# Loading the input transposed, warming TensorE ahead of the first products, and four small edits in a one-core diffusion step

## The chip, the cores and the metric

The kernel runs on one core of a Trainium2 chip. The metric is device time in microseconds (us). The kernel before takes 435.55 us, the median of 3 runs (435.24 to 435.67). The profile shown below is of one further execution that took 436.31 us, of which the profiler's span covers 434.5 us.

## What is computed

One layer of a hybrid mixer works on 640 tokens of 1024 channels: 128 context tokens and 512 latent tokens. Cut to what this change touches, the reference is

```python
mod = silu(c) @ w_ada + b_ada                  # c_ctx for context, c for latent tokens
shift, scale, gate = split(mod, 3)
h = rmsnorm(x, g_pre) * (1 + scale) + shift    # 640 x 1024
proj = h @ w_in                                # 3840 columns: qa ka va ga qr zf zb ir gr uf gf
# neighbourhood attention (8 heads), bidirectional gated recurrence (4 heads), Fourier mixing,
# each times a gate taken from proj, then
y = x + gate * rmsnorm(mixed @ w_out, g_post)
```

The outputs are y, the new keys and values of the context tokens, and the final states of the recurrence. The scale and shift that a channel gets depend only on which of the two groups its token belongs to, so they are two numbers a channel each.

## The kernel before

Everything is float32. A weight or vector that goes into a big product is split into a high part (rounded to the fast float32 format, by ScalarE) and a low part (the rest, by VectorE), and a product is the sum of three fast products: high by high, high by low, low by high (`mm3`, line 210). In the products the channels lie on the partitions, in KT = 8 tiles of 128 channels; `hT[0]` and `hT[1]` (line 203) hold the high and low parts of the modulated input, 128 channels by 640 tokens for each of the 8 tiles.

**The first stage** is `start_stream` (line 244). It loads x as five tiles of 128 tokens, each in a piece of 640 columns (`xa`) and one of 384 (`xb`), on SyncE's queue, and behind them the 16 modulation weights `wss` of 512 KB, with the first two blocks of the input projection (`win`) in between. `scale_x` (line 222) takes the sum of squares of a token from ScalarE (line 225) and VectorE (line 226), its root and reciprocal (lines 164 and 165), and scales the tile (lines 230 and 231). Then, for each channel tile k:

- `mod_cols` (line 195) forms scale and shift of 128 channels from two weight blocks, as 8 narrow products each (128x32 by 128x128, two records of the profile for one product);
- VectorE copies the result out of PSUM into `row` (line 266), TensorE transposes it (line 270), VectorE adds up (line 272) and makes `G` (lines 273 and 274) and `shift` (line 275);
- `modulated` (line 233) transposes five 128x128 pieces of x on TensorE into PSUM, ScalarE applies `G` and `shift` to them (line 237 for the latent tokens, line 239 for the context tokens), and VectorE writes the high part (line 240) and the low part (line 241) of `hT`.

`zf_stream` (line 283) follows tile by tile: 12 products of 320 columns for each k, into four PSUM banks, which `gate` (line 321) empties with two sigmoids each when the eighth k is in. `fill` (line 958) starts after the fifth tile and runs all other blocks of the projection in a list, one block being 48 such products.

**The later stages** overlap: two recurrences (`recurrence`, line 416; VectorE updates over seven levels, then the states, line 525), four attentions, the Fourier part and the output projection. `attention_blocks(p)` (line 574) projects values, transposes the five 128-token tiles of the values with `by_token` (line 343) into two PSUM banks, four tiles in a bank of the kind "b" and the fifth in one of the kind "f" (of which there are three, and in which the blocks accumulate), and splits them into `vs` (line 632). The gate of the output is made in `gate_vectors` (line 846), which uses a small constant `sel`.

**What sets the order.** The functions are generators; a planner (`Order`) with estimated costs interleaves them, and that gives the program order. Within it the framework's scheduler orders each engine's instructions by a simulated timeline. SyncE's loads are chained in the order of `wdma`; each engine's queue runs strictly in its order. SyncE has up to eight loads under way and then waits for an earlier one to land.

Of the kernel before, what the change touches and what calls it, by code (L numbers as in the profile page):

```python
# [9 lines left out]
F32 = mybir.dt.float32  # L10
# [3 lines left out]
ALU = mybir.AluOpType  # L14
# [3 lines left out]
P = 128  # L18
# [53 lines left out]
def mixer_kernel(ctx: ExitStack, tc: tile.TileContext, A, O):  # L72
# [51 lines left out]

    def tr(out, src):
        od.now += 0.107
        last_tr[0] = te.transpose(out, src, ident).ins  # L127

    def split(src, hi, lo, hi_eng=None, lo_eng=None):
        (sc.copy if hi_eng is None else hi_eng.tensor_copy)(hi, src)  # L130
        (ve if lo_eng is None else lo_eng).tensor_sub(lo, src, hi.bitcast(F32))  # L131
# [41 lines left out]
    wdma, nb = [], [1]  # L173
# [7 lines left out]
    def split_w(raw, lo_eng=None, shape=(KT, P), tags=("hi", "lo")):  # L181
        hi, lo = [wp.tile([P, *shape], F32R, tag=t, name=nm(t), bufs=WB[t]) for t in tags]
        split(raw, hi, lo, lo_eng=lo_eng)
        return hi, lo
# [10 lines left out]
    def mod_cols(out, w, chain):  # L195

        t = od.now
        for k in range(KT):
            run_mm(chain, out[32 * (k % 4):32 * (k % 4) + 32, :], csil[:, k, :], w[:, k, :], start=(k < 4), stop=(k >= 4))
        od.now = t + 0.45  # L200
# [3 lines left out]
    xa, xb = [T(tag="xa") for _ in range(5)], [T(384, tag="xb") for _ in range(5)]  # L204

    def xcols(i, k):
        return (xa[i] if k < 5 else xb[i])[:, k % 5 * P:k % 5 * P + P]
# [9 lines left out]
    def load_x():  # L217
# [4 lines left out]
    def scale_x():  # L222
        for i in range(5):
            ss2 = S(2)
            sc.activation(T(), xa[i], ACT.Square, accum_out=ss2[:, 0:1])
            ve.tensor_tensor_reduce(PE_()[:, 0:384], xb[i], xb[i], 1.0, 0.0, op0=ALU.mult, op1=ALU.add,
                                    accum_out=ss2[:, 1:2])
            ve.tensor_add(rstd[:, i:i + 1], ss2[:, 0:1], ss2[:, 1:2])
            rsqrt_mean(rstd[:, i:i + 1], D)
            ve.tensor_scalar(xa[i], xa[i], rstd[:, i:i + 1], 0.0, op0=ALU.mult, op1=ALU.add)  # L230
            ve.tensor_scalar(xb[i], xb[i], rstd[:, i:i + 1], 0.0, op0=ALU.mult, op1=ALU.add)

    def modulated(k, pm):
        h, px = T(), PB()
        for i in range(1, 5):
            tr(px[:, (i - 1) * P:i * P], xcols(i, k))
        sc.activation(h[:, P:NT], px, ACT.Identity, bias=shift[:, k, 1:2], scale=G[:, k, 1:2])
        tr(pm[:, 384:512], xcols(0, k))
        sc.activation(h[:, 0:P], pm[:, 384:512], ACT.Identity, bias=shift[:, k, 0:1], scale=G[:, k, 0:1])
        ve.tensor_copy(hT[0][:, k, :], h)  # L240
        ve.tensor_sub(hT[1][:, k, :], h, hT[0][:, k, :].bitcast(F32))
        od.set(f"h{k}", LAT["h"])

    def start_stream():
        load_x()
# [10 lines left out]
        scale_x()  # L256
        od.now = 11.0
        for k in range(KT):
# [7 lines left out]
            ve.tensor_copy(row, pm[:, 0:256])  # L266
            yield LAT["row"]

            for u in range(2):
                tr(pm[:, u * P:(u + 1) * P], row[:, u * P:(u + 1) * P])  # L270
            pt = S(4)
            ve.reduce_sum(pt, pm[:, 0:256].rearrange("p (u g r) -> p u r g", u=2, r=32)[:, :, 0:2, :], axis=AX.X)
            ve.tensor_scalar(G[:, k, :], pt[:, 0:2], bss[:, k, 0:1], 1.0, op0=ALU.add, op1=ALU.add)
            ve.tensor_scalar_mul(G[:, k, :], G[:, k, :], gpre[:, k:k + 1])  # L274
            ve.tensor_scalar_add(shift[:, k, :], pt[:, 2:4], bss[:, k, 1:2])
            modulated(k, pm)
# [66 lines left out]
    def by_token(src):  # L343
# [4 lines left out]
        return [(slice(4 * j, 4 + j), pt[j][:, 0:(4, 1)[j] * P].rearrange("p (i e) -> p i e", e=P)) for j in range(2)]  # L348
# [225 lines left out]
    def attention_blocks(p):  # L574
# [54 lines left out]
        vp = by_token(vT)  # L629
# [216 lines left out]
    def gate_vectors():  # L846
        selr = cp.tile([P, 2, P], F32R, tag="selr", name="selr")
# [219 lines left out]
def prepare(inp):  # L1067
    inp = {k: np.asarray(v) for k, v in inp.items()}
    r = _consts()
    r["x"] = np.concatenate([inp["x_prompt"][0], inp["x_sample"][0]], 0)  # L1070
    r["cc"] = np.stack([inp["c_ctx"], inp["c"][0]], -1).reshape(KT, P, 2).transpose(1, 0, 2)
# [59 lines left out]
```

## Time and profile before

| | |
|---|---|
| median of 3 runs | 435.55 us |
| profiled execution | 436.31 us, span 434.5 us |
| TensorE busy (modelled) | 410.3 us, 94% |
| VectorE busy | 303.2 us, 70% |
| ScalarE busy | 204.7 us, 47% |
| first product of TensorE | 14.27 us |
| read from memory | 43.80 MB |

PE is TensorE, PEld its weight loads, DVE VectorE, ACT ScalarE, POOL GpSimd, SP SyncE. In the groups of instructions a row reads: line, engine, operation, output<-input, shapes, count | busy time, mean ns of one | idle time of the engine just ahead of it and what ended that. The rows by stretch of time give, for each engine, the busy time and the count of instructions, then the granted clock of TensorE, the busy share of the DMA engines and GB/s. The chain of waits is followed back from the last instruction; a row there is a start, a length and the engine with the tile it writes. In the timeline the first two columns are start and length, and a bracket tells how long the engine had been idle and what released it.

### The profile page before, as it was taken

The numbers are of one execution on the slowest core, as the hardware profiler recorded it, in microseconds if no ns is written. First come the engines' busy times: TensorE is split into PE (matmuls) and PEld (weight loads), VectorE is DVE, ScalarE is ACT, GpSimd is POOL, SyncE is SP. The second block draws the span as 40 slices with busy tenths as digits, with TensorE's granted clock in tenths as the row PEclk, the third lists the DMA queues.
The fourth block names the chain that finished last, engine by engine and source line by source line (L and its number), as shares of the span: only waits on it lengthen the run. The fifth ranks groups of instructions, "written<-read, shape, count | busy, mean of one in ns | idle before, by whom it ended". The sixth has DMA issues, their size and how long they took to land.

```text
span 434.5 us, 8311 instructions
## 1 busy us (share of the span) xinstructions
PE 410.3 (94%) x3176; PEld 373.0 (86%) x3176; DVE 303.2 (70%) x866; ACT 204.7 (47%) x546; POOL 7.4 (2%) x23
## 2 busy tenths in 40 slices
PE   0699999999998999999999999999999999999994
PEld 0388899999988998999899989899898889988884
DVE  2775479999986865885597658786679748471164
ACT  5524467575341525654454534744456553251231
POOL 2000000000020100000000000000000000000000
PEclk9999999999999999999999999999999999999999
DMA  7996143211202011132112423245324203245032
GB/s 241 411 407 228 49 154 116 66 55 50 84 23 74 13 60 50 56 97 66 40 61 67 146 67 92 93 152 181 100 55 141 98 1 105 76 160 205 0 146 98
DMA packets 19528, 47.62 MB, mean 110 GB/s; under 512 B 3184, under 2 KB 6912, under 8 KB 19488
## 3 DMA queue, kind: packets, MB, share of 16 engines
q1 hardware_dynamic: 19376, 46.94, 31.7%
q8 instruction: 25, 0.41, 0.4%
q0 software_dynamic: 112, 0.14, 0.3%
q14 instruction: 15, 0.12, 0.1%
HBM read 43.80 MB, written 3.28 MB: 108 GB/s over the span
## 4 chain that ended last, share of the span: by engine, by line
PE 90%; DVE 4%; DMA 3%; ACT 1%; issue 1%; SPq 0%; DVEq 0%; ACTq 0%
PE pb L113 83%; PE pb L127 6%; DMA vs<-wss 1%; DMA txa<-x 1%; DVE AL L451 1%; DVE t L525 1%; DVE AL L488 0%; ACT L681 0%; DVE lo L131 0%; DVE t L953 0%; ACT hi L130 0%; ACT pe L682 0%; DVE t L468 0%; DVE t L467 0%; DVE AC L451 0%
## 5 line engine op out<-in xcount | busy, mean ns | idle before, releaser
L113 PE MATMUL pb<-hT,hi 128*128 128x320 f32 x896 | 209.5, 317 | 3.0 <-DVE vs L131 1.5
L113 PEld LDWEIGHTS pb<-hT,hi 128*128 128x128 f32 x896 | 149.4, 188 | 9.5 <-issue 2.3
L113 PE MATMUL pb<-hT,lo 128*128 128x320 f32 x448 | 139.0, 312 | 0.0
L113 PEld LDWEIGHTS pb<-hT,lo 128*128 128x128 f32 x448 | 84.1, 188 | 1.0 <-DVE G L274 0.2
L131 DVE TENSOR_TENSOR lo<-raw,hi 128x1024 fp32r<-128x1024 f32 x35 | 42.8, 1223 | 26.9 <-ACT hi L130 26.5
L130 ACT CAST hi<-raw 128x1024 fp32r<-128x1024 f32 x35 | 36.8, 1051 | 41.9 <-PE pb L113 20.9
L113 PE MATMUL pb<-t,t 64*128 64x128 f32 (+2 forms) x414 | 43.1, 291 | 0.4 <-DVE AL L451 0.4
L113 PEld LDWEIGHTS pb<-t,t 64*128 64x128 f32 (+1 forms) x414 | 36.2, 188 | 4.8 <-issue 0.8
L130 ACT CAST pT<-pb 128x256 fp32r<-128x256 f32 x64 | 23.3, 372 | 19.3 <-DVE pT L131 12.3
L113 PE MATMUL pb<-hi,mh 128*128 128x512 f32 (+1 forms) x108 | 32.1, 376 | 0.0
L131 DVE TENSOR_TENSOR pT<-pb,pT 128x256 fp32r<-128x256 f32 x64 | 26.4, 418 | 1.7 <-ACT pT L130 1.5
L113 PEld LDWEIGHTS pb<-hi,mh 128*128 128x128 f32 x108 | 19.4, 189 | 3.2
L113 PE MATMUL pb<-pT,mh 128*128 128x512 f32 (+1 forms) x102 | 22.2, 364 | 0.0
L681 ACT ACTIVATE pe<-pb,s 128x256 f32<-128x256 f32 x32 | 15.3, 477 | 13.8 <-DVE s L680 7.9
L127 PE MATMUL pb<-ident,pe 128*128 128x128 f32 x136 | 20.9, 273 | 0.5 <-ACT pe L682 0.5
L113 PEld LDWEIGHTS pb<-pT,mh 128*128 128x128 f32 x102 | 17.7, 189 | 3.1
L936 ACT ACTIVATE t<-pb 128x512 f32<-128x512 f32 (+1 forms) x11 | 6.0, 551 | 30.1 <-PE pb L113 30.1
L113 PE MATMUL pb<-lo,mh 128*128 128x512 f32 (+1 forms) x54 | 20.2, 373 | 0.0
L127 PEld LDWEIGHTS pb<-ident,pe 128*128 128x128 f32 x136 | 16.6, 140 | 1.4 <-ACT pe L682 0.7
L451 DVE COPY_PREDICATED AL<-masks,pb 128x512 f32<-128x512 uint32 x24 | 16.5, 738 | 1.5 <-PE pb L113 1.5
L113 PE MATMUL pb<-pT,vs 128*128 128x256 f32 (+1 forms) x96 | 16.8, 321 | 0.0
L113 PE MATMUL pb<-vs,csil 128*32 128x128 f32 x64 | 3.3, 335 | 14.3 <-DMA vs<-wss 14.3
(205 smaller groups left out, 636.3 us busy)
## 6 DMA issues: line engine op xcount, KB each, us to landing
raw<-win SPq DMA_DIRECT2D x30, 512.0 KB, 3.5
pT<-wss SPq DMA_DIRECT2D x12, 512.0 KB, 10.2
raw<-wg SPq DMA_DIRECT2D x8, 512.0 KB, 3.5
raw<-wout SPq DMA_DIRECT2D x8, 512.0 KB, 3.5
t<-x SPq DMA_DIRECT2D x10, 256.0 KB, 6.1
o_y<-t SPq DMA_DIRECT2D x9, 256.0 KB, 2.1
vs<-wss SPq DMA_DIRECT2D x4, 512.0 KB, 9.3
tbl<-tbl SPq DMA_DIRECT2D x4, 512.0 KB, 3.5
```

The costliest lines, as they stand in the source:

```text
L113: return te.matmul(out, lhsT, rhs, start=start, stop=stop).ins
L127: last_tr[0] = te.transpose(out, src, ident).ins
L130: (sc.copy if hi_eng is None else hi_eng.tensor_copy)(hi, src)
L131: (ve if lo_eng is None else lo_eng).tensor_sub(lo, src, hi.bitcast(F32))
L451: ve.copy_predicated(out, mk.to_broadcast([P, i1 - i0, P]), src)
L525: ve.scalar_tensor_tensor(sall[r, cdst], sall[r, cs], Td[r, ip:ip + 1], pst[r, cdst], op0=ALU.mult, op1=ALU.add)
L681: sc.activation(pe[:, 256:512], ss[:, 256:512], ACT.Exp, bias=m[:, 1:2], accum_out=m[:, 3:4])
L936: sc.activation(T(512)[:, cs], po[:, 0:cs.stop - cs.start], ACT.Square, accum_out=ssb[:, j:j + 1])
```

## The change

- The input is handed over a second time, transposed (`xT`, 8 tiles of 128 channels by 640 tokens), and this is what the first stage loads. The five TensorE transposes for each channel tile are gone. x itself is still loaded, by tokens, for the last addition.
- `inverse_norms` squares the eight tiles on ScalarE, adds them up on VectorE (`acc`), and sums over the partitions with five products against a 128x2 tile of ones. `spread_norms` transposes the reciprocal roots, broadcast along the free dimension, so that every partition holds all 640 of them (`rb`, copied out of PSUM by ScalarE). Each `xT[k]` is multiplied by `rb` on VectorE.
- `modulated` applies `G` and `shift` to `xT[k]` in SBUF. The high part is copied by VectorE for k of 0 and 1, by ScalarE after that.
- Ahead of it all, TensorE makes 36 transposes of the identity whose result nobody reads.
- A number of instructions of the first tiles are tied to a stated order (`turn`): the order binds them on their engine, without a wait of its own.
- `G` is made in one VectorE instruction from a prepared scale bias plus 1 (`bsc1`).
- At k = 5 a sigmoid of one column, whose result nobody reads, is put on ScalarE, so that the table of the gate is loaded there.
- `cc` and `lbl` are loaded on ScalarE's queue, `xT` first of all on SyncE's, `sel` behind the weights on SyncE's instead of on GpSimd's.
- In `attention_blocks` the fifth value tile is copied by ScalarE from its PSUM bank into an SBUF tile (of the kind "m", four buffers), and the splits read the copy.

```diff
-    cc = const("cc", [KT, 2], dma=sy.dma_start)
-    lbl = const("lbl", [2, 2], dma=sy.dma_start)
+    xT, x_last = [], None
+    for k in range(KT):
+        xT.append(T(tag="xT"))
+        with tc.issue_after(x_last) if x_last else ExitStack():
+            x_last = sy.dma_start(xT[k], A["xT"][k]).ins
+    lbl = const("lbl", [2, 2], dma=sc.dma_start)
+    cc = const("cc", [KT, 2], dma=sc.dma_start)
     bss = const("bss", [KT, 2])
     gpre = const("gpre", [KT])
-    sel = const("sel", [2, P])
+    bsc1 = const("bsc1", [KT])
+    ve.tensor_scalar(bsc1, bss[:, :, 0], 1.0, 0.0, op0=ALU.add, op1=ALU.add)
+    ones = cp.tile([P, 2], F32, tag="ones", name="ones")
+    ve.memset(ones, 1.0)
...
+    pr = PB()
+    for i in range(36):
+        te.transpose(pr[:, i % 4 * P:i % 4 * P + P], ident, ident)
+
+    def inverse_norms():
+        acc = T()
+        sc.activation(acc, xT[0], ACT.Square)
+        for k in range(1, KT):
+            sq = T()
+            sc.activation(sq, xT[k], ACT.Square)
+            ve.tensor_add(acc, acc, sq)
+        pn = PB()
         for i in range(5):
-            load(xa[i], A["x"][i * P:(i + 1) * P, 0:NT])
-            load(xb[i], A["x"][i * P:(i + 1) * P, NT:D])
+            mm(pn[:, 2 * i:2 * i + 2], acc[:, i * P:(i + 1) * P], ones)
+        sc.activation(rstd, pn[:, 0:10].rearrange("p (i two) -> p i two", two=2)[:, :, 0], ACT.Sqrt, bias=eps, scale=1.0 / D)
+        ve.reciprocal(rstd, rstd)
+        return pn
+
+    def spread_norms(pn, prev):
+        for i in range(5):
+            tr((pr if i < 4 else pn)[:, i % 4 * P:i % 4 * P + P], rstd[:, i:i + 1].to_broadcast([P, P]))
+            if i == 0:
+                turn_names(last_tr[0], prev)
+        rb = T()
+        sc.copy(rb[:, 0:512], pr)
+        return rb, sc.copy(rb[:, 512:NT], pn[:, 0:P])
+
+    def modulated(k):
+        h = T()
+        sc.activation(h[:, P:NT], xT[k][:, P:NT], ACT.Identity, bias=shift[:, k, 1:2], scale=G[:, k, 1:2])
+        h_act[0] = sc.activation(h[:, 0:P], xT[k][:, 0:P], ACT.Identity, bias=shift[:, k, 0:1], scale=G[:, k, 0:1])
+        if k < 2:
+            h_hi[0] = ve.tensor_copy(hT[0][:, k, :], h)
+        else:
+            sc.copy(hT[0][:, k, :], h)
+        return ve.tensor_sub(hT[1][:, k, :], h, hT[0][:, k, :].bitcast(F32))
...
             for u in range(2):
-                mod_cols(pm[:, u * P:(u + 1) * P], raws[2 * k + u], [])
+                chain = []
+                mod_cols(pm[:, u * P:(u + 1) * P], raws[2 * k + u], chain, row_tr)
+            if k == 0:
+                rb, rb_act = spread_norms(pn, chain[-1])
             yield 0
-            ve.tensor_copy(row, pm[:, 0:256])
+            row_copy = ve.tensor_copy(row, pm[:, 0:256])
+            if k:
+                turn(row_copy, row_done)
+            if k == 0:
+                turn(ve.tensor_mul(xT[0], xT[0], rb), row_copy)
...
+            row_done = ve.tensor_scalar(G[:, k, :], pt[:, 0:2], bsc1[:, k:k + 1], gpre[:, k:k + 1], op0=ALU.add, op1=ALU.mult)
+            h_done = modulated(k)
+            if k + 1 < KT:
+                turn(ve.tensor_mul(xT[k + 1], xT[k + 1], rb), row_done)
             if k < 2:
-                zf_w.append(split_w(zraw[k]))
+                zf_w.append(split_w(zraw[k], prev=rb_act, lo_prev=h_hi[0] if k == 0 else h_done))
+                rb_act, row_done = h_act[0], h_done
...
+            if k == 5:
+                sc.activation(S(1), G[:, k, 0:1], ACT.Sigmoid)
...
-        return [(slice(4 * j, 4 + j), pt[j][:, 0:(4, 1)[j] * P].rearrange("p (i e) -> p i e", e=P)) for j in range(2)]
+        last = pt[1][:, 0:P]
+        if copy_last:
+            last = S(P)
+            sc.copy(last, pt[1][:, 0:P])
+        return [(slice(4 * j, 4 + j), (pt[0], last)[j].rearrange("p (i e) -> p i e", e=P)) for j in range(2)]
```

More of the change, by code (lines that the diff above doesn't have):

```diff
@@ L123, in run_mm, with turn_names, turn @@
         chain.append(ins)
+    def turn_names(ins, prev):
+        tc.add_manual_dep(ins, prev.name, mybir.DependencyInfo(mybir.DependencyClass.NoSync, mybir.DependencyReason.DATA),
+                          reason="turns")
+    def turn(ins, prev):
+        turn_names(ins.ins, prev.ins)
+        return ins
     def tr(out, src):
@@ L127, in tr, with split @@
         last_tr[0] = te.transpose(out, src, ident).ins
-    def split(src, hi, lo, hi_eng=None, lo_eng=None):
-        (sc.copy if hi_eng is None else hi_eng.tensor_copy)(hi, src)
-        (ve if lo_eng is None else lo_eng).tensor_sub(lo, src, hi.bitcast(F32))
+    def split(src, hi, lo, hi_eng=None, lo_eng=None, prev=None, lo_prev=None):
+        ins = (sc.copy if hi_eng is None else hi_eng.tensor_copy)(hi, src)
+        if prev is not None:
+            turn(ins, prev)
+        ins = (ve if lo_eng is None else lo_eng).tensor_sub(lo, src, hi.bitcast(F32))
+        if lo_prev is not None:
+            turn(ins, lo_prev)
     ident = cp.tile([P, P], F32, tag="ident", name="ident")
@@ L193, in load, with mod_cols @@
             sy.dma_start(t, src)
-    def mod_cols(out, w, chain):
+    def mod_cols(out, w, chain, prev=None):
         t = od.now
@@ L199, in mod_cols @@
             run_mm(chain, out[32 * (k % 4):32 * (k % 4) + 32, :], csil[:, k, :], w[:, k, :], start=(k < 4), stop=(k >= 4))
+            if k == 0 and prev is not None:
+                turn_names(chain[0], prev)
         od.now = t + 0.45
@@ L215, in mixer_kernel @@
     HF = (slice(0, 320), slice(320, 640))
-    def load_x():
-        for i in range(5):
-            load(xa[i], A["x"][i * P:(i + 1) * P, 0:NT])
-            load(xb[i], A["x"][i * P:(i + 1) * P, NT:D])
-    def scale_x():
-        for i in range(5):
[L224 to L241, printed above, removed]
+    pr = PB()
@@ L255, in start_stream @@
             loads(k)
-        scale_x()
+        pn = inverse_norms()
         od.now = 11.0
+        row_tr, row_done = None, None
         for k in range(KT):
@@ L270, in start_stream @@
                 tr(pm[:, u * P:(u + 1) * P], row[:, u * P:(u + 1) * P])
+            row_tr = last_tr[0]
             pt = S(4)
             ve.reduce_sum(pt, pm[:, 0:256].rearrange("p (u g r) -> p u r g", u=2, r=32)[:, :, 0:2, :], axis=AX.X)
[L273 to L274 removed]
             ve.tensor_scalar_add(shift[:, k, :], pt[:, 2:4], bss[:, k, 1:2])
[L276 removed]
+            row_done = ve.tensor_scalar(G[:, k, :], pt[:, 0:2], bsc1[:, k:k + 1], gpre[:, k:k + 1], op0=ALU.add, op1=ALU.mult)
+            h_done = modulated(k)
+            if k + 1 < KT:
+                turn(ve.tensor_mul(xT[k + 1], xT[k + 1], rb), row_done)
             if k < 2:
[L278 removed]
+                zf_w.append(split_w(zraw[k], prev=rb_act, lo_prev=h_hi[0] if k == 0 else h_done))
+                rb_act, row_done = h_act[0], h_done
             if k == 1:
                 od.set("zw", 0.0)
+            if k == 5:
+                sc.activation(S(1), G[:, k, 0:1], ACT.Sigmoid)
             yield max(0.0, 13.5 + 2.7 * (k + 1) - od.now)
@@ L628, in attention_blocks @@
         yield next(q_gen)
-        vp = by_token(vT)
+        vp = by_token(vT, True)
         for hh in range(2):
@@ L846, in gate_vectors @@
     def gate_vectors():
+        sel = const("sel", [2, P], dma=load)
         selr = cp.tile([P, 2, P], F32R, tag="selr", name="selr")
```

14 lines of the change are left out of this document (6 added, 8 removed).

## The prediction, made before the result was known

> **What bounds the kernel now.** I read the page's shares first, then the busy times by stretch, then the chain of waits of the first 35 us, then the groups of instructions that the change touches.
>
> ```profile
> PE 410.3 (94%) x3176; PEld 373.0 (86%) x3176; DVE 303.2 (70%) x866; ACT 204.7 (47%) x546; POOL 7.4 (2%) x23
> ```
> ```profile
> 0.00:10.00 10.00, 0.00 (x0) 0.00 (x0) 2.42 (x13) 5.48 (x9) 3.08 (x11) 1.00 0.74 227
> ```
> ```profile
> 14.27:23.40 9.13, 8.92 (x90) 5.57 (x94) 6.72 (x19) 3.51 (x5) 0.00 (x0) 1.00 1.03 410
> 23.40:51.63 28.23, 28.23 (x344) 25.52 (x337) 16.94 (x50) 9.11 (x15) 0.00 (x0) 1.00 0.62 238
> 51.63:53.80 2.17, 1.17 (x8) 0.90 (x7) 0.00 (x0) 2.09 (x4) 0.00 (x0) 1.00 0.00 0
> 53.80:119.30 65.50, 65.49 (x562) 62.26 (x562) 60.79 (x139) 39.02 (x91) 0.00 (x0) 1.00 0.27 86
> 119.30:134.20 14.90, 13.06 (x119) 11.48 (x118) 13.22 (x41) 6.22 (x16) 2.42 (x6) 1.00 0.07 24
> 134.20:428.60 294.40, 293.45 (x2067) 267.26 (x2065) 197.07 (x586) 134.93 (x394) 1.91 (x6) 1.00 0.28 90
> ```
>
> TensorE is the bound from its first product to 428.6 us: between 53.8 and 428.6 us it idles 0.01 + 1.84 + 0.95 = 2.8 us in all. So a microsecond is won only where TensorE starts earlier, works faster, has less to do or waits less, and nearly all of that lies ahead of 53.8 us.
>
> ```profile
> 8.31 5.82 DMA vs<-wss
> ...
> 14.27 1.08 PE pb L113 x16
> ...
> 21.22 0.51 DVE hT L240
> 21.77 2.34 PE pb L113 x20
> ...
> 27.21 1.01 PE pb L113 x32
> ...
> 28.92 1.76 PE pb L113 x12
> 30.68 0.22 PE pb L127 x2
> ```
>
> The chain runs over loads until 14.27 us. Then 16 narrow records take 1.08 us, while from 27.21 us on 32 of them take 1.01 us: the array works at half speed at first, although the granted clock reads 1.00 in the row from 14.27 to 23.40. The first product of 320 columns comes at 21.77 us, and soon after the speed doubles. Full-speed prices follow: a narrow record 1.01/32 = 0.0316 us, a 320-column product 1.76/12 = 0.147, a transpose 0.22/2 = 0.11.
>
> ```profile
> L113 PE MATMUL pb<-hT,hi 128*128 128x320 f32 x77 | 18.4, 327 | 0.1
> L113 PE MATMUL pb<-hT,lo 128*128 128x320 f32 x37 | 11.1, 314 | 0.0
> L113 PE MATMUL pb<-pT,csil 128*32 128x128 f32 x192 | 8.4, 311 | 0.0
> L127 PE MATMUL pb<-ident,txa 128*128 128x128 f32 x25 | 5.6, 339 | 0.0
> L127 PE MATMUL pb<-ident,row 128*128 128x128 f32 x16 | 3.5, 301 | 0.1
> L113 PE MATMUL pb<-vs,csil 128*32 128x128 f32 x64 | 3.3, 335 | 14.3 <-DMA vs<-wss 14.3
> L127 PE MATMUL pb<-ident,txb 128*128 128x128 f32 x15 | 2.5, 276 | 0.0
> ```
>
> These are TensorE's groups up to 51.7 us. At full speed they are worth 114 x 0.147 + 256 x 0.0316 + 56 x 0.11 = 16.8 + 8.1 + 6.2 = 31.1 us. They end at 51.63, so 20.5 us are lost there: 14.3 before the first product and 6.2 to half speed and stalls. About 5 of the 6.2 fall before 23.4 us, where the nine microseconds hold some four microseconds of full-speed work; about 1.2 fall after it.
>
> **The change part by part.**
>
> Work removed: 25 + 15 transposes of x, 40 x 0.11 = 4.4 us, counted at full speed because slowness is booked in the 20.5. Added: five products against ones and five transposes of the norms (0.55 us). The nearest row to the former is five products of the same kind with two columns, 1.28 us:
>
> ```profile
> 120.73 1.28 PE L113 MATMUL pb<-bones,t 128*128 128x2 f32 x10
> ```
>
> So the work up to the same point becomes 31.1 - 4.4 + 1.8 = 28.5 us. The 36 identity transposes end before the first weights: 36 x 0.22 at half speed is 7.9 us, from about 3.4 us on, when the identity is made. Only loads are on the path then, so they cost nothing.
>
> ```profile
> 3.10 0.29 POOL masks.py:199 TENSOR_SCALAR_AFFINE_SELECT ident<-ident 128x128 f32<-128x128 f32 x1
> ```
>
> When the weights land.
>
> ```profile
> 1.65 0.42 SPq L193 DMA_DIRECT2D txa<-x  x1
> ```
> ```profile
> cc<-cc SPq DMA_DIRECT2D x1, 8.0 KB, 1.7
> ```
>
> The first x load is issued at 1.65 us now, behind cc and lbl, which go to ScalarE's queue, so it goes out at 0.73, 0.92 us earlier. sel (131 KB, 0.32 us at the 410 GB/s of the second stretch) leaves this time. The first weight block, landing at 14.13, would come at 12.9. If the loads also ran at 410 GB/s from 2.4 us on (0.73 and the 1.7 that 8 KB take to land), the bytes of x and of the first block would be through at 2.4 + 3.15 MB/410 = 10.1. Today 2.27 MB are through at 10 us and the 3.3 MB up to this block at 12.5, so the landing lags by 1.6 us: 11.7. I take 12.3; every further 512 KB takes 1.28 us: second block 13.6, fourth 17.4 (a zf block lies between), last x tile 11.0.
>
> ```profile
> L237 ACT ACTIVATE t<-pb,shift,G 128x512 f32<-128x512 f32 x8 | 6.2, 779 | 17.4 <-DVE G L274 17.4
> L239 ACT ACTIVATE t<-pb,shift,G 128x128 f32<-128x128 f32 x8 | 3.6, 455 | 3.1 <-PE pb L127 3.1
> L225 ACT ACTIVATE t<-txa 128x640 f32<-128x640 f32 x5 | 3.6, 726 | 2.7 <-DMA txa<-x 2.6
> ...
> L164 ACT ACTIVATE rstd<-rstd,eps 128x1 f32<-128x1 f32 x5 | 1.4, 288 | 1.3 <-DVE rstd L228 1.3
> ```
> ```profile
> L241 DVE TENSOR_TENSOR hT<-t,hT 128x640 fp32r<-128x640 f32 x8 | 6.6, 823 | 0.2
> L240 DVE CAST hT<-t 128x640 fp32r<-128x640 f32 x8 | 3.9, 491 | 5.0 <-ACT t L239 5.0
> L266 DVE COPY row<-pb 128x256 f32<-128x256 f32 x8 | 3.4, 421 | 1.6 <-PE pb L113 1.6
> L273 DVE TENSOR_SCALAR G<-s,bss 128x2 f32<-128x2 f32 x8 | 1.8, 227 | 0.2
> ...
> L425 DVE TENSOR_TENSOR t<-t,t 128x640 f32<-128x640 f32 x2 | 1.6, 814 | 0.0
> ```
>
> The first vector. From the last x tile at 11.0: square 0.73, addition 0.81 (12.6), products with ones 1.28 (13.9), root 0.29 and a reciprocal no longer than that (14.4); the modulation of k = 0 is through by 14.1, so the norms are spread by 15.0; two copies out of PSUM, at most the 1.24 of lines 237 and 239 (16.2); multiplication 0.81 (17.0); ScalarE 0.78 + 0.46 (18.3); high part 0.49: 18.8 us, against 21.77 now. By then TensorE has done the norms (1.8), both tiles' modulation (64 records, 2.0) and a pair of transposes (0.2): 4.0 us of work, 14.8 lost.
>
> After the first vector. The zf block of p = 1 and the second vector are not ready at once (wss3 at 17.4, then much the same steps): I take 1.5 us of waiting. Then a tile costs TensorE 32 x 0.0316 + 0.22 + 1.76 = 3.0 us and VectorE 0.42 + 0.23 x 3 + 0.81 + 0.82 = 2.7, and the loads 2.56 for two blocks. Three paces this close will get in each other's way a little; I add the 1.2 us of today's later part and 0.5 for it. ScalarE, with 0.78 + 0.46 + 0.73 = 2.0 a tile, hides the high parts moved to it. The load of the gate's table at k = 5 is covered by products still queued at TensorE; without that cover it is the 1.28 us below and a short instruction. Lost: 14.8 + 1.5 + 1.2 + 0.5 = 18.0; end of the same work: 28.5 + 18.0 = 46.5, against 51.63, a gain of 5.1 us. The bounds are 16.0 lost (no waiting beyond today's) and, with the loads 0.6 later and the table uncovered, 20.0.
>
> The turns add no waits; queued behind the instructions they hold are VectorE's next row copy and, through it, the next tile's modulation. cc and lbl on ScalarE's queue have until 12.3 us. sel, on SyncE's, pushes the later weights by 0.32, within the bounds.
>
> The gate's table.
>
> ```profile
> 51.70 1.28 ACT L325 ACT_TABLE_LOAD   x1 [2.08 <-PE pb L113]
> ...
> 53.81 0.56 PE L113 MATMUL pb<-hT,hi 128*128 128x320 f32 x2 [1.02 <-ACT t L326]
> ```
>
> TensorE waits for the bank that two sigmoids empty after a 1.28 us load. With the load gone they end at about 52.5, when TensorE has run dry at about 52.6 anyway: gain 1.1 (0.9 to 1.2).
>
> The copied value tile.
>
> ```profile
> 133.50 0.21 DVE L131 TENSOR_TENSOR vs<-pb,vs 128x64 fp32r<-128x64 f32 x1
> 133.74 0.59 DVE L525 SCALAR_TENSOR_TENSOR t<-t,m,pb 64x64 f32<-64x64 f32 x2
> 133.86 0.53 PE L113 MATMUL pb<-hT,hi 128*128 128x320 f32 x2 [1.48 <-DVE vs L131]
> ```
>
> TensorE waits 1.48 us for a bank whose last reader is the low part of `vs`. The copy would free it at once, but it needs a fifth buffer of a kind that has four, all held by the two recurrences (`Tf` and `Tb` of each) until the first one's last line 525, at about the same 134 us. So the wait stays with another cause: I take 0, between a gain of 1.5 and a loss of 0.6.
>
> Sum for the profiled execution: 436.31 - 5.1 - 1.1 - 0 = 430.1. The median of the runs lies 0.76 below that execution, so 429.3.
>
> [...]
>
> **The rivals.**
>
> The warm-up does not take (0.28). Either the transposes do not raise the speed, or it falls again in the 3 us between their end and the first weights. [...] Price: on the way to the first vector one block's modulation (+0.5), the products with ones (+0.5), five transposes (+0.5), and another pair (+0.2) are slow; after it the speed is low for the 1.6 us from 21.77 to 23.4, 0.8 lost. 2.4 less gain: 431.7.
>
> All goes well (0.15): lost only 16.0, and the bank freed at once. 7.1 + 1.1 + 1.5 = 9.7 less: 425.8.
>
> The middle takes it back (0.07). VectorE is busy 60.79 of 65.50 us up to 119.3; if its recurrence does not start earlier, TensorE arrives earlier and waits. Against it: what starts it comes from TensorE. Only the table's gain stays: 434.4.
>
> Slower (0.08): a tile becomes serial. VectorE now has a multiplication by `rb` and the row copy in a stated order, and ScalarE the high part. If a row copy had to wait for the low part of the tile before, a tile would take 0.42 + 0.4 + 0.23 x 3 + 0.81 + 1.24 + 0.73 + 0.82 = 5.1 us (0.4 for the pair of transposes and its hops). The eighth vector would come at 18.8 + 7 x 5.1 = 54.5 and its products end at 56.3; 0.9 of that can be filled with six products of the next block's first half, so the end is 3.8 later than 51.63, 2.7 with the table: 438.2. It decides from 4.7 us a tile. Against it: the scheduler may put the next row copy ahead of the low part.
>
> **How the numbers follow.** The forecast, warm and paced as summed, has 0.42: 429.3. The range goes from the second rival's 425.8 to 433.5, the first rival's 431.7 with 1.2 of the bounds on loads and table and 0.6 of the copy; what it leaves out is the middle and the slower case, 0.15, and edges. What a measurement here can tell from no change is 0.2%, 0.9 us. The first three cases (0.85) and half of the middle's are faster by more: 0.88. The rest of the middle's and a little of the slower one's lie within: 0.05. Slower: 0.07.
>
> **What would show it.** Right: the first block's 16 records take near 0.55 us, not 1.08; the first 320-column product starts near 18.8 us; the zf sums end 5 us earlier for the same count of products; no table load stands at the gates and TensorE's gap there is under 0.3 us; near 128 us TensorE still waits at the value tile, for a copy that waits for line 525. The first rival shows as 1.08 us again; the slower one as a distance of over 4.7 us between high parts; the middle as idle time of TensorE between 53 and 134 us that grows by what was won. I would be wrong altogether if the scheduler laid out the later stages differently, since 2.8 us of idle time there leave little to win and much to lose.

## The result and the profile after

| | before | after |
|---|---|---|
| median, same chip | 435.39 us (4 runs, 435.09 to 435.67) | 439.86 us (4 runs, 438.91 to 439.92) |
| profiled execution, span | 436.31, 434.5 | 439.92, 438.1 |

The ratio is 1.0098, 95% interval 1.0086 to 1.0111: 4.5 us slower, where 6.1 us faster was forecast. The ratios and intervals, here and below, leave out three executions that took 525, 1013 and 1335 us, two of the kernel before and one of b_table_copy. The line numbers below are those of the changed kernel unless another is named: 113 the products, 136 the transposes, 139 and 142 the high and low parts of a weight, 240 the transposes of the identity, 249 the sum of squares, 305 the row copy, 309 and 321 the multiplications by `rb`, 271 to 278 `modulated`, 329 the early sigmoid, 578 the former 525.

First the shares, and the rows by stretch of time (engine busy times, granted clock, share of the DMA engines, GB/s).

```profile
PE 415.4 (95%) x3187; PEld 379.2 (87%) x3187; DVE 303.6 (69%) x840; ACT 211.2 (48%) x553; POOL 7.3 (2%) x22
```
```profile
0.00:9.60 9.60, 6.30 (x36) 6.06 (x36) 2.82 (x11) 6.12 (x10) 2.22 (x9) 1.00 0.80 277
9.60:14.20 4.60, 0.00 (x0) 0.00 (x0) 4.13 (x5) 3.17 (x5) 0.00 (x0) 1.00 1.03 417
14.20:16.20 2.00, 1.98 (x10) 1.98 (x10) 0.00 (x0) 0.00 (x0) 0.00 (x0) 0.57 1.02 408
16.20:20.00 3.80, 3.80 (x44) 2.93 (x48) 0.72 (x3) 1.01 (x4) 0.00 (x0) 0.50 1.03 410
20.00:25.00 5.00, 2.67 (x37) 1.91 (x29) 4.46 (x9) 3.09 (x5) 0.20 (x1) 0.84 1.03 405
25.00:30.00 5.00, 3.90 (x41) 3.19 (x42) 2.18 (x7) 1.20 (x2) 0.19 (x1) 0.69 0.72 271
30.00:35.00 5.00, 4.42 (x24) 3.50 (x27) 2.28 (x5) 0.00 (x0) 0.00 (x0) 0.66 1.00 365
35.00:51.63 16.63, 15.58 (x228) 13.55 (x221) 12.24 (x29) 11.79 (x18) 0.00 (x0) 1.00 0.39 141
...
57.20:124.00 66.80, 66.80 (x577) 63.45 (x577) 60.89 (x139) 39.54 (x93) 0.00 (x0) 1.00 0.27 88
```

From 57 us on TensorE is as full as before. All of the loss lies ahead of it: holes in its work, most of them between 9.6 and 35 us and 1.05 us more up to 51.63, and a low clock from 14 to 35 us. The product on `bones`, a landmark behind the first stage, tells the size: it stood at 120.73 us and stands at 124.82, 4.1 us later. The two profiled executions differ by 3.6 us, so a little is won behind `bones`; the small edits below show where.

```profile
124.82 1.28 PE L113 MATMUL pb<-bones,t 128*128 128x2 f32 x10
```

Next the groups up to 51.7 us.

```profile
L113 PE MATMUL pb<-hT,hi 128*128 128x320 f32 x57 | 15.2, 351 | 4.1 <-DVE hT L274 2.5 <-DVE hT L278 1.6
L113 PE MATMUL pb<-hT,lo 128*128 128x320 f32 x27 | 9.1, 350 | 0.3 <-DVE lo L142 0.3
```

By 51.7 us TensorE has run 84 products of 320 columns against 114 before, although it had forty transposes less to do. Then TensorE's and VectorE's timelines (start, length, and in brackets how long the engine had been idle and what released it).

```profile
3.21 6.30 PE L240 MATMUL pb<-ident 128*128 128x128 f32 x36 [3.21 <-POOL ident masks.py:199]
...
14.22 2.09 PE L113 MATMUL pb<-ones,t 128*128 128x2 f32 x10 [4.72 <-DVE t L249]
16.24 1.08 PE L113 MATMUL pb<-vs,csil 128*32 128x128 f32 x16
17.09 1.08 PE L113 MATMUL pb<-pT,csil 128*32 128x128 f32 x16
18.10 1.33 PE L136 MATMUL pb<-ident,rstd 128*128 128x128 f32 x5
19.22 0.63 PE L136 MATMUL pb<-ident,row 128*128 128x128 f32 x2
...
23.01 0.97 PE L113 MATMUL pb<-hT,hi 128*128 128x320 f32 x4 [1.43 <-DVE hT L274]
...
26.64 0.63 PE L136 MATMUL pb<-ident,row 128*128 128x128 f32 x2
...
34.11 0.63 PE L136 MATMUL pb<-ident,row 128*128 128x128 f32 x2
```
```profile
7.75 6.41 DVE L249 TENSOR_TENSOR t<-t,t 128x640 f32<-128x640 f32 x7 [1.60 <-ACT t L248]
...
22.46 0.49 DVE L274 CAST hT<-t 128x640 fp32r<-128x640 f32 x1 [0.54 <-ACT t L272]
22.87 1.22 DVE L142 TENSOR_TENSOR lo<-raw,hi 128x1024 fp32r<-128x1024 f32 x1
24.00 0.82 DVE L278 TENSOR_TENSOR hT<-t,hT 128x640 fp32r<-128x640 f32 x1
24.74 0.41 DVE L305 COPY row<-pb 128x256 f32<-128x256 f32 x1
```

Three things are to be read here. The transposes of the identity end at 9.51 us, and TensorE stands still for 4.72 us until the squares are summed. The products with ones come first in TensorE's queue and keep the modulation, whose weights are there, waiting until 16.24; all of it runs at half speed again (1.08 us for 16 records, a granted clock of 0.50 from 16.20 us on). And the row copy of the second tile, at 24.74, comes behind the low part of the first tile (24.00), which comes behind the 1.22 us for the low part of a weight: the row transposes of the first three tiles stand at 19.22, 26.64 and 34.11, 7.4 us a tile. Part of the 7.4 is TensorE's: the second row copy ends at 25.15, but its transposes stand in the queue behind products of the first tile, at half speed (a granted clock of 0.50), until 26.64.

The late points: TensorE's waits, and the load of the gate's table on ScalarE.

```profile
PE pb L113 <- DVE t L249: 4.7, 1, 4.7
PE pb L113 <- DVE hT L274: 2.5, 2, 1.4
PE pb L113 <- DVE hT L278: 1.6, 3, 0.9
PE pb L113 <- DVE t L578: 1.5, 1, 1.5
```
```profile
46.52 1.28 ACT L329 ACT_TABLE_LOAD   x1
```

The table is loaded early, as meant. The rows show TensorE busy for 66.80 of 66.80 us from 57.20 on, so no gap is left at the gates. The wait at the last value tile is still 1.5 us, with the recurrence's line 578 as its cause: ScalarE's copy of the tile (line 400) waits 6.0 us for that line, as the prediction said.

### The profile page after: what moved, and what is told of

It is laid out like the page before. It is cut to its first block, busy times and chain, and to the rows that moved or that the text cites. A ratio compares the mean times of both kernels' runs of the same rounds, so it can differ in the third digit from the quotient of the medians.

```text
span 438.1 us, 8294 instructions
## 1 busy us (share of the span) xinstructions
PE 415.4 (95%) x3187; PEld 379.2 (87%) x3187; DVE 303.6 (69%) x840; ACT 211.2 (48%) x553; POOL 7.3 (2%) x22
## 4 chain that ended last, share of the span: by engine, by line
PE 84%; DVE 6%; DMA 6%; ACT 2%; issue 1%; DVEq 0%; SPq 0%; ACTq 0%
PE pb L113 79%; PE pb L136 5%; DMA pT<-wss 2%; DMA txT<-xT 1%; DMA raw<-win 1%; DVE lo L142 1%; DMA lbl<-lbl 1%; DVE t L578 1%; DVE AL L504 1%; ACT t L271 1%; DVE hT L278 1%; ACT hi L139 0%; DVE txT L321 0%; DVE AL L541 0%; ACT L734 0%
## 5 line engine op out<-in xcount | busy, mean ns | idle before, releaser
L113 PE MATMUL pb<-hT,lo 128*128 128x320 f32 x448 | 140.6, 316 | 0.3 <-DVE lo L142 0.3
L113 PEld LDWEIGHTS pb<-hi,mh 128*128 128x128 f32 x108 | 19.4, 189 | 3.2
L745 DVE TENSOR_TENSOR o<-pb,o 64x512 f32<-64x512 f32 (+1 forms) x16 | 7.8, 487 | 13.5 <-ACT o L744 13.4
```

What stands on the lines that cost most here:

```text
L113: return te.matmul(out, lhsT, rhs, start=start, stop=stop).ins
L745: ve.tensor_add(out, src[r, :], out)
```

## The experiments

The first theory: the changed first tiles are serial, because a tie (a stated order between two instructions) puts the row copy behind the low part. Beside it stand two others. One is that the products with ones block TensorE's queue (theory 2 in the expectations), the other that TensorE's speed falls back since the transposes end too early (theory 3). All kernels were timed against the kernel before on the same chip:

| kernel | median | before | ratio, 95% interval | `bones` at |
|---|---|---|---|---|
| after | 439.86 | 435.39 | 1.0098 (1.0086 to 1.0111) | 124.82 |
| a_row_free | 436.11 | 435.20 | 1.0021 (1.0010 to 1.0031) | 121.06 |
| a_warm80 | 436.92 | 435.20 | 1.0035 (1.0019 to 1.0052) | 122.38 |
| a_norm_late | 437.99 | 435.20 | 1.0062 (1.0040 to 1.0083) | 122.63 |
| a_all_three | 434.76 | 435.20 | 0.9998 (0.9982 to 1.0014) | 119.96 |
| a_early | 435.32 | 435.46 | 0.9992 (0.9981 to 1.0003) | 119.21 |
| a_spread | 434.87 | 435.46 | 0.9988 (0.9976 to 1.0000) | 121.26 |
| a_no_norm | 432.33 | 435.46 | 0.9926 (0.9901 to 0.9951) | 117.76 |
| a_no_ties | 441.54 | 435.46 | 1.0137 (1.0119 to 1.0155) | 125.61 |
| a_light_three | 437.39 | 435.36 | 1.0037 (1.0006 to 1.0069) | 123.39 |
| b_table | 434.81 | 435.46 | 0.9983 (0.9971 to 0.9995) | 118.92 |
| b_copy | 434.98 | 435.46 | 0.9982 (0.9969 to 0.9995) | 119.19 |
| b_table_copy | 433.99 | 435.46 | 0.9965 (0.9953 to 0.9977) | 117.90 |
| b_warm74 | 436.61 | 435.46 | 1.0041 (1.0024 to 1.0057) | 120.45 |
| b_light | 434.69 | 435.36 | 0.9986 (0.9976 to 0.9995) | 119.61 |
| b_light_warm | 434.78 | 435.36 | 0.9998 (0.9984 to 1.0012) | 119.02 |

Kernels a_ start from the changed one, kernels b_ from the one before. `bones` is from one profiled execution each, which need not stand at the median: that of b_table_copy took 432.05 us. It moves by up to 1 us with the landing of the first weights alone: the wait for them is 14.3 us in the profile of before, 14.0 in that of b_table, 13.7 in that of b_copy, 13.3 in that of b_table_copy, with the same first loads.

**The tie alone** (a_row_free).

```diff
-                rb_act, row_done = h_act[0], h_done
+                rb_act = h_act[0]
```

> The changed kernel (439.9 us), but the row copies of tiles 1 and 2 are ordered only behind the G of the tile before, no longer behind its low part. Theory 1 (the stated order makes the first tiles serial: the chain from low part to row copy to transposes to the next vector): first-to-third vector distance falls from about 7.5 us a tile to under 5, time falls by 3 to 5 us, to 435 to 437. Theory 2 (the five products with ones stand at the head of TensorE's queue and hold up the modulation) and theory 3 (the array has fallen back to half speed when the products begin): at most 1 us, 439 to 440.

It stands 0.9 us above its before instead of 4.5: 3.6 us for one line. Its row transposes, in TensorE's timeline:

```profile
19.43 0.64 PE L136 MATMUL pb<-ident,row 128*128 128x128 f32 x2
...
22.52 0.44 PE L136 MATMUL pb<-ident,row 128*128 128x128 f32 x2 [1.43 <-DVE row L305]
...
27.56 0.38 PE L136 MATMUL pb<-ident,row 128*128 128x128 f32 x2
```

The distance between tiles falls from 7.4 us to 3.1 and 5.0. So the serial tile is shown.

**All ties dropped** (a_no_ties).

```diff
     def turn_names(ins, prev):
-        tc.add_manual_dep(ins, prev.name, mybir.DependencyInfo(mybir.DependencyClass.NoSync, mybir.DependencyReason.DATA),
-                          reason="turns")
+        return
```

> The changed kernel with all stated orders dropped, so that the scheduler alone orders the first tiles. Theory 1 (one tie, row copy behind the low part, does the harm): like the kernel with that tie alone dropped, 435.5 to 436.5. If the other ties help: 437 or more. If they harm as well: under 435.

It is 1.6 us worse than the change, 6.1 above its before; the first product of 320 columns comes at 29.07. Against a_row_free, which drops the one tie alone, it is 5.4 us worse: the other ties together are worth that much. Which of them matter was not tried one by one.

**A longer warm-up** (a_warm80).

```diff
-    for i in range(36):
+    for i in range(80):
```

> The changed kernel with 80 unused transposes in place of 36, so that they last until about 13 us. Theory 3: the products with ones and the modulation run at full speed from the start (16 records in 0.55 us, not 1.08), time falls by 2 to 3 us, to 437 to 438. Theories 1 and 2: the speed is full but the chain on VectorE and the loads are as long: under 1 us. If transposes do not raise the speed at all: no change in the records.

It is 2.8 us better than the change, measured above each one's before. TensorE's rows by stretch:

```profile
14.20:20.00 5.80, 4.45 (x84) 3.54 (x82) 2.78 (x8) 2.90 (x6) 0.00 (x0) 1.00 1.03 408
20.00:25.00 5.00, 3.34 (x12) 2.55 (x12) 2.70 (x4) 1.20 (x2) 0.27 (x1) 0.66 1.03 406
```

Until 20 us the clock reads 1.00 and 84 records fit where the change had 10 + 44. Then the serial tiles leave holes again, and from 20 to 25 us the clock reads 0.66.

**The products with ones behind the first modulation** (a_norm_late).

```diff
-        return pn
+    def root_norms(acc, prev):
...
+            ins = mm(pn[:, 2 * i:2 * i + 2], acc[:, i * P:(i + 1) * P], ones)
+            if i == 0:
+                turn_names(ins, prev)
...
+                pn = root_norms(acc, chain[-1])
```

> The changed kernel with the five products with ones placed on TensorE behind the modulation of the first tile. Theory 2: the first modulation starts near 12 us and not at 16.2, and the time falls by 2 to 4 us, to 436 to 438. Theories 1 and 3: the first vector still waits for the norms (the sum on VectorE ends at 14.2 us), so under 1 us is won.

The modulation now starts at 11.66 us, and the time is 1.7 us better. **All three** (a_all_three: the diffs of a_row_free, a_warm80 and a_norm_late together):

> All three edits together: row copies free of the low part, 80 transposes, products with ones behind the first modulation. If the three theories cover the loss: 429 to 432, near the 429.3 forecast for the change. If over 434, something else holds the first stage back (the paces of the three engines, or the buffers of the weights).

It is 4.9 us better than the change and equal to the kernel before; alone the three add up to 8.0, so they overlap. Its first product still comes at 22.80 us, and the rows by stretch say why:

```profile
14.20:20.00 5.80, 5.28 (x91) 4.21 (x89) 1.93 (x9) 1.16 (x4) 0.00 (x0) 1.00 1.02 407
20.00:25.00 5.00, 2.20 (x20) 1.83 (x24) 5.00 (x8) 4.04 (x6) 0.36 (x1) 0.77 1.04 406
```

In the second row VectorE is busy for all of the 5 us and TensorE for 2.2: three multiplications by `rb` run from 20.05 to 22.3 us, ahead of the first high part at 22.26. In a_warm80 and in a_norm_late the first of them ran at 18.2 us and the first product came at 20.84. Here the 80 transposes last until 14.99, and the modulation of two tiles stands ahead of the spreading of the norms in TensorE's queue.

**The way over the norms.** a_early has all three edits with 60 transposes, and the silu of `cc` written behind the squares. On ScalarE the silu still ran first (6.38 us), so that half did not take effect.

> The three edits together with 60 transposes in place of 80 (they end near 12.5 us, not 14.9) and the silu of c put behind the squares on ScalarE, so that these start when the first x tile lands, near 4 us, and not at 6.4. If the rest of the loss lies in the way to the first vector (sum on VectorE done at 14.2 us against a forecast of 12.6, transposes standing in front of the modulation): the sum ends near 12.5, the first 320-column product comes near 20.5 us and not 22.8, and the time falls by 2 us, to 432.5 to 433.5. If the first stage is held by its pace a tile: 434.5 to 435.

The sum still ends at 14.3 us. The first product comes at 20.38, as expected, but the time is 435.3 and not 432.5 to 433.5. One of the ten executions took 433.05, with a mean granted clock of 0.997; the other nine had 0.984 to 0.989 and took 434.9 to 435.7. The profiled one is of the nine. Its row from 134 to 138 us, and below it the same stretch of a_all_three:

```profile
134.00:138.00 4.00, 4.00 (x23) 4.00 (x21) 2.10 (x7) 0.00 (x0) 0.00 (x0) 0.62 0.22 57
134.00:138.00 4.00, 4.00 (x34) 4.00 (x33) 2.86 (x8) 0.70 (x1) 0.00 (x0) 1.00 0.04 10
```

From `bones` on TensorE runs the same 2164 records in the same order in both, and both wait 1.5 us at the value tile just ahead of this row. Yet the clock fell in one and not in the other, and a_early is 1.6 us longer from there to the last product.

a_spread frees the row copy and takes the sum to TensorE (products against a 128x128 tile of ones), so that no transposes and PSUM copies of norms are left:

```diff
+            for u in range(2):
+                mm(pn[u][:, 0:320], onesr, sq[:, HF[u]], start=(k == 0), stop=(k == KT - 1))
...
+            act = sc.activation(rb[:, HF[u]], pn[u][:, 0:320], ACT.Sqrt, bias=eps, scale=1.0 / D)
+        ve.reciprocal(rb, rb)
```

> The changed kernel with row copies free of the low part and the way of the norms shortened: the eight squares go to TensorE as fast-float32 products against a 128x128 tile of ones, which sum over the channels and spread the sum to all partitions at once; root and reciprocal work on the spread 128x640 sum. No additions on VectorE, no transposes of the norms. Three unused transposes follow each square, to keep TensorE busy. Theory 4 (what is left of the loss is the serial way from the last x tile to the first vector, 23.0 us in the change against 18.8 forecast): the first 320-column product comes near 16 to 18 us and the time is 431 to 433.5. If the first stage is held by its pace a tile after the first vector: 434 to 435.

The sum is done 14.2 us into the span, but the reciprocal of the wide tile eats what that brings. The first product comes at 22.89 and not near 16 to 18. VectorE's timeline:

```profile
15.23 4.15 DVE L256 RECIPROCAL t<-t 128x640 f32<-128x640 f32 x1 [8.49 <-ACT t L255]
```

a_no_norm frees the row copy, has 60 transposes, and leaves the norms out of the computation:

```diff
-        acc = T()
-        sc.activation(acc, xT[0], ACT.Square)
...
+        rb = T()
+        ve.memset(rb, 1.0)
+        return rb
```

> The changed kernel with row copies free of the low part and 60 unused transposes, and the norms left out of the computation (rb is a constant 1, the multiplications by it stay). This bounds what the way of the norms costs. Theory 4: the first 320-column product comes near 16 us and the time is 430 to 432. If the pace a tile holds the stage: 433.5 to 435, as with the norms in.

It stands 3.1 us under its before, where a_early was 0.1 under its own: 3.0 us between them. Not all of that belongs to the norms. In the two profiled executions, which stand near the medians, the first product comes at 18.88 (near 16 was expected) against 20.38 and `bones` at 117.76 against 119.21, so the norms cost about 1.5 us in the first stage; the other 1.5 is the fall of the clock in a_early behind `bones`. Even without the norms half of the forecast gain is missing. Rows by stretch of a_no_norm:

```profile
14.20:20.00 5.80, 3.39 (x52) 1.84 (x52) 4.43 (x9) 2.88 (x4) 0.00 (x0) 0.86 1.03 409
20.00:25.00 5.00, 4.62 (x42) 3.86 (x42) 1.98 (x6) 1.40 (x3) 0.11 (x1) 0.50 1.03 406
```
```profile
PE pb L113 <- DMA pT<-wss: 2.1, 3, 0.9
```

The first tiles now wait for weights, 2.1 us in three waits, and the clock falls again, to 0.86 and then 0.50.

**The small edits, alone in the kernel before.** b_table has the first two lines of this, b_copy the rest, b_table_copy both.

```diff
+            if k == 5:
+                sc.activation(S(1), G[:, k, 0:1], ACT.Sigmoid)
...
+        last = pt[1][:, 0:P]
+        if copy_last:
+            last = S(P)
+            sc.copy(last, pt[1][:, 0:P])
...
-        vp = by_token(vT)
+        vp = by_token(vT, True)
```

> The kernel before with the early sigmoid at k = 5 alone. By the prediction's price, 1.1 us less: 434.1. If the table load at k = 5 is not covered, as in the changed kernel where it stands 1.5 us in ScalarE's way between the vector and its high part, the gain is eaten: 435 to 436.

> The kernel before with the copied value tile alone. By the prediction the wait at 133.9 us stays with another cause (the copy needs a buffer that the recurrence holds): 435.0 to 436.2, no change. If the copy does free the bank at once, 1.5 us less, 433.9.

> The kernel before with the early table load and the copied value tile, without the new input. Each alone moved the time by 0.2%; if they add up, 0.3 to 0.4% less, near 434.0; if one of the two was chance, 0.1 to 0.2% less.

The table gives 0.17% (0.05 to 0.29%), about 0.7 us, and the copy 0.18% (0.05 to 0.31%). Together they give 0.35%: the fastest here of the kernels that compute the whole result, ahead of a_all_three, which has the same two edits and the new first stage. In b_table's profile the wait of 1.0 us at the gates is gone. In b_copy's profile the wait at the value tile is as long as ever:

```profile
PE pb L113 <- DVE t L529: 1.5, 1, 1.5
```

So the copy does not win there. The traces show where it does: from the start of `bones` to the start of TensorE's last product the five kernels without the copy take 307.5 to 307.6 us, and eleven of the twelve with it 306.1 to 306.8 (a_early, with its lower clock, 307.8). The 2164 records and the waits (2.8 us) are the same in before and b_copy, but the scheduler has put the records in another order, and TensorE runs through that order 1.2 us sooner. Six of b_copy's twelve executions had a mean granted clock of 0.992 or 0.993 and took 435.2 to 436.0; the other six, with 0.996 to 0.999, took 433.3 to 434.8.

**Half speed in the kernel before** (b_warm74, line numbers its own).

```diff
+    pr = PB()
+    for i in range(74):
+        te.transpose(pr[:, i % 4 * P:i % 4 * P + P], ident, ident)
```

> The kernel before with 74 unused transposes alone, lasting until about 14 us. Theory 3 (the transposes do raise the speed, and in the change they only end too soon): the first 16 narrow records take 0.65 us and not 1.08, and of the 5 us that the slow start costs 2 to 4 are won: 431.5 to 433.5. [...]

It is not faster, but slower by 0.4%. Its first products, its stretches ahead of 51.63 us and its waits:

```profile
14.50 0.64 PE L113 MATMUL pb<-vs,csil 128*32 128x128 f32 x16
...
21.11 0.56 PE L113 MATMUL pb<-hT,hi 128*128 128x320 f32 x2 [0.39 <-DVE hT L244]
```
```profile
14.50:23.40 8.90, 6.97 (x99) 4.49 (x102) 7.11 (x19) 3.39 (x5) 0.00 (x0) 1.00 1.03 409
23.40:51.63 28.23, 27.73 (x338) 24.67 (x330) 15.45 (x46) 9.25 (x16) 0.00 (x0) 1.00 0.62 240
```
```profile
PE pb L127 <- DVE row L270: 0.7, 2, 0.5
PE pb L113 <- DMA pT<-wss: 0.6, 1, 0.6
PE pb L113 <- DVE lo L131: 0.5, 1, 0.5
PE pb L113 <- DVE hT L244: 0.4, 1, 0.4
PE pb L113 <- ACT hi L130: 0.2, 1, 0.2
```

Full speed is there, and TensorE now waits 2.4 us in six waits where before it waited for nothing: the speed turned into waits, 1.6 us of them for VectorE. Part of VectorE's time goes back to a load in turn. VectorE's addition for the first tile (18.61) stands behind the low part of a weight. That one waits for its high part on ScalarE, and the high part waits for the weight to land:

```profile
16.39 1.04 ACT L130 CAST hi<-raw 128x1024 fp32r<-128x1024 f32 x1 [1.72 <-DMA raw<-win]
```
```profile
17.46 1.23 DVE L131 TENSOR_TENSOR lo<-raw,hi 128x1024 fp32r<-128x1024 f32 x1 [0.89 <-ACT hi L130]
```

The transposes themselves also last too long: they end at 14.56, while the first weights landed at 13.8. Of the 1.2 us between the medians the profile shows nothing, for the profiled execution took 436.03 us, less than that of before (436.31). The times of all twelve executions tell more: five had a mean granted clock of 0.988 to 0.994 and took 437.5 to 439.0 us, the other seven, with 0.996 to 0.999, took 435.7 to 436.8. The kernel before had 0.995 to 0.999. Where the clock fell in the five, no trace shows.

Whether the loads were behind it all was tried by leaving out the odd ones of the sixteen modulation weights:

```diff
-                raws.append(load_raw(A["wss"][2 * k + u], RAW[2 * k + u]))
+                raws.append(raws[-1] if u else load_raw(A["wss"][2 * k], RAW[2 * k]))
```

> The kernel before with only the even ones of the sixteen modulation weight blocks loaded, each used for scale and shift alike, so 4.2 MB less are loaded and the scale is computed from the wrong block. The forecast counted some 5 us ahead of 23.4 us as lost to TensorE's half speed; b_warm74 won none of them. Theory that loads set the pace of the first stage: the first product of 320 columns comes earlier than 21.77 us by about the 1.28 us of one block, the sums of zf end some 3 us earlier, the time is about 432. Rival, that VectorE and the hops from engine to engine set it: the first product moves by under 1.3 us, the time by under 1 us.

> b_light with the 74 unread transposes ahead. If the half speed of the first products was hidden by loads alone, it now shows: faster than b_light by 1.5 us or more, against the 1.2 us that the same transposes cost in b_warm74. If VectorE and the hops pace the stage, the transposes bring less than 1 us here too.

> a_all_three (row copies free, 80 transposes, products with ones behind the first modulation) with only the even weight blocks loaded, each used for scale and shift alike. Its first product of 320 columns stands at 22.80 us, 4.0 later than forecast. Theory that the way over the norms sets it, and not loads: the first product stays within 1 us of 22.80, and the time falls by under 2 us from 434.8. Rival, that loads hold the first tiles: the first product comes 1.3 us earlier or more and the time is 431 or less.

4.2 MB less brought 0.7 us, and the transposes on top of that nothing in time. The first product of b_light came at 23.33, later than the 21.77 of before and not earlier. So the theory that loads set the pace did not come out as expected. TensorE's waits ahead of 51.63 us in b_light_warm are 1.6 us for weight blocks and 0.9 for VectorE:

```profile
13.86 1.08 PE L113 MATMUL pb<-vs,csil 128*32 128x128 f32 x32
...
19.62 1.08 PE L113 MATMUL pb<-vs,csil 128*32 128x128 f32 x32 [1.40 <-DMA vs<-wss]
...
22.73 0.86 PE L113 MATMUL pb<-hT,hi 128*128 128x320 f32 x4 [0.46 <-DVE hT L244]
```

The way from the first modulation, through at 14.9, to this product takes 7.8 us there, at full speed and with half the weights. But these kernels also have another order of the tiles, since the scheduler plans with the loads that it sees: three tiles are modulated ahead of the first product, where the kernel before has two. So they do not say what fewer loads would bring in the order of before; that stays open. a_light_three, whose executions spread from 433.8 to 439.9 us, was 2.6 us slower than a_all_three, with a first product at the same place (22.83 against 22.80) and a new hole at 35.6 us, where a vector's high part on ScalarE stands behind that of a weight that has not landed; that is a matter of the order, too.

## Why the prediction was wrong

**What bounds the kernel: held.** TensorE is full from 57 us on, and what was lost ahead of it came out at the end: `bones` 4.1 us later, the profiled execution 3.6 and the median 4.5.

**"The turns add no waits": the step that failed at the highest price.** The prediction named what is queued behind the tied instructions, VectorE's next row copy and through it the next tile's modulation, and then priced that at nothing. The rival "slower" described just this: a row copy that waits for the low part of the tile before. I gave it 0.08, because the scheduler "may put the next row copy ahead of the low part"; yet the diff's line `rb_act, row_done = h_act[0], h_done` and `turn(row_copy, row_done)` forbid exactly that for the row copies of the second and third tile. The answer stood in the diff. That the rival's 438.2 us came near the 439.86 is luck: it took seven distances of 5.1 us, and there were two of 7.4, since the low part of a weight (1.22 us), which it left out, stands in the same queue, and TensorE ran at half speed. Taking the tie away gives back 3.6 us.

**The way to the first vector: mis-sized, and one wait overlooked.** Forecast and found, in us:

| step | forecast | found |
|---|---|---|
| squares summed | 12.6 | 14.16 |
| products with ones through | 13.9 | 16.3 |
| modulation of k = 0 through | 14.1 | 18.2 |
| norms spread | 15.0 | 19.4 |
| `rb` copied | 16.2 | 20.0 |
| first product of 320 columns | 18.8 | 23.01 |

The sum priced only the last tile's square and addition after its load. But seven additions, one every 0.92 us (6.41/7), run one behind the other from 7.75 us on, and the squares before them wait for the silu of `cc` and its table. The first x tile landed 3.1 us after its issue at 0.73, but its square ran at 6.38. The prediction gave `cc` on ScalarE's queue until 12.3 us, as the modulation needs it then; it overlooked that the silu stands ahead of the squares. What an earlier silu would bring was not measured, since a_early did not move it.

The modulation was counted as done beside the products with ones, but it is queued behind them, which take 2.1 us. Half speed, at which the products with ones take 2.09 us and 16 records of the modulation 1.08 (1.28 and 0.64 in a_warm80), is the second half of the first rival: the speed did take and then fell. The prediction let TensorE wait for weights after the transposes; it waits for the sum. a_warm80 gives back 2.8 us, near the 2.4 that this rival was priced at.

**"About 5 of the 6.2" lost to half speed: not won.** The prediction took slow work as time to be won. In the kernel before, b_warm74 made that work fast (the first 16 records in 0.64 us) and TensorE waited instead, mostly for VectorE, so that almost nothing was ahead later (`bones` 0.3 us earlier, and no gain in the time). What holds VectorE in turn, its own pace, the order of its queue or the loads behind it, is not separated. A ledger of one engine says what is lost, not what another engine lets one win.

**Moving the norms: a cost that was missing.** By tokens, each tile's norm was made while the next was loading. With channels on the partitions no norm exists until all eight tiles are in, and then sum, products, root, spreading, copying and multiplying come one after another. The forecast had these steps, but weighed them against 21.77 us rather than asking what they would put on VectorE. a_no_norm puts them at about 1.5 us by `bones`.

**The gate's table: held.** The forecast was 1.1 us (0.9 to 1.2), a little more than the 1.02 us of TensorE's gap in its own row; alone the edit wins 0.7 us (0.2 to 1.3). In the changed kernel no gap is left there; the last one, 0.37 us at 55.58, is a wait for the high part of the last tile. **The copied tile: held** in what was said of the wait. Its 0.18% lies within the bounds of the sum, but the value taken was 0, and it comes from the order of TensorE's later work, which the prediction did not consider.

**What is closed and what is open.** Of the 10.6 us between forecast and result, the three edits give back 4.6 to 4.9 (a_early, a_all_three). Leaving the norms out takes the time another 3.0 us down from a_early: about 1.5 for the norms, about 1.5 for the later fall of the clock. The last 3.0 lie behind the first product, which a_no_norm has at 18.88 us, as forecast (18.8). From its first row transposes to the second it takes 7.2 us (15.47 to 22.67), and from 20 to 25 us the granted clock is 0.50, where the forecast had 3.0 us a tile at full speed and 1.5 us of waiting. How much of this is the clock and how much the order in the queues was not measured. b_table_copy, with the two small edits and the old first stage, stands at 0.9965; a_all_three, with the same edits and the repaired new stage, at 0.9998. So the new first stage, even when repaired, is 1.0 to 1.4 us slower than the old one.

## What to carry to other kernels

A tie between two instructions prices at whatever its later one has queued behind it: follow that to the next tile, and read in the diff which orders it forbids. Slow or idle time of the bound engine is won only as far as the next engine allows, so before counting it, take the pace of the second engine in the same stretch. And moving a reduction to the other axis is worth only what is left after the time at which its first result can exist.

## What the runs showed of the hardware

- TensorE's speed rose while it ran transposes one behind the other. In the changed kernel the 36 float32 transposes take 6.30 us; by the starts of their records 21 run at 0.21 us each and the rest at 0.11, so the speed rose after 4.5 us. In the other kernels with such transposes it rose, estimated from their totals at these two paces, after 3.2 us (a_row_free, 36 in 5.70 us) to 5.8 us (b_warm74, 74 in 11.11 us). Behind the 80 of a_warm80 the first 16 narrow records took 0.64 us, and the granted clock was 1.00 from 14.20 to 20.00 us.
- Narrow products and transposes in turn ran slowly for longer: in the kernel before they fill TensorE from 14.27 to 21.77 us, with 0.2 us of gaps, and five transposes at 19.37 still took 1.33 us; four at 23.95, behind the first products of 320 columns, took 0.60.
- After idle time the speed was lower: in the changed kernel 4.72 us without work were followed by a granted clock of 0.57 and then 0.50.
- It also fell without one long gap: in a_no_norm TensorE's longest wait from 13 to 20 us was 0.92 us, with 3.39 of 5.80 us busy from 14.2 us on, and in the 5 us after that, 4.62 of them busy, the granted clock was 0.50.
- The clock differed between two executions of the same work: from `bones` on a_early and a_all_three give TensorE the same records in the same order, and after the same wait of 1.5 us the granted clock from 134 to 138 us was 0.62 in one and 1.00 in the other.
- The granted clock read 1.00 over slow work: in the changed kernel the row of the first 9.6 us reads 1.00 although 21 transposes took 0.21 us each, against 0.11 for those that follow.
- A reciprocal on VectorE cost 4.15 us for 128x640 (a_spread), 6.5 ns an element of a partition, where an addition of that shape takes 0.82; for 128x5 it took 0.19 (the changed kernel).
